# One attention pair ahead: moving the sliding-window attention of a hybrid decoder layer in front of the recurrence it used to run beside

## The chip, the cores and the metric

The kernel runs on one core of a Trainium2 chip. Its time is the device time of one execution in microseconds (us); three runs of the kernel before gave 2196.97, 2198.31 and 2198.78, so a median of 2198.31. The engines are PE (TensorE: matrix multiplications and transposes), DVE (VectorE), ACT (ScalarE), POOL (GpSimd) and SP (SyncE, which here only issues DMAs). Each works through its own queue in order, and semaphores tie them together. A change of 0.2% of the time, 4.4 us, is about what the measurement can tell from none.

## The reference

One layer on 2048 positions of width 1024, in float32. Two groups of heads read the same normed input and are concatenated; a gated MLP with a causal convolution follows.

```python
u = rmsnorm(h, norm_mix_w)
proj = u @ w_in
# 4 recurrent heads (HGRN2) of width 128: q, f, value, output gate
f = lb + (1 - lb) * sigmoid(hf);  k = 1 - f
S_t = diag(f_t) S_{t-1} + k_t v_t^T;  o_t = S_t^T q_t
o_hg = rmsnorm(o, hg_norm_w) * silu(hg)
# 8 attention heads of width 64 (2 key/value heads), window of 128, a sink logit each
o_att = softmax over own and previous 128-key block, plus sink
h = h + concat(o_hg, o_att) @ w_out
v = rmsnorm(h, norm_ffn_w)
gate = causal_depthwise_conv(v @ w_gate)
h = h + (silu(gate) * (v @ w_up)) @ w_down
out = rmsnorm(h, final_norm_w)
```

## The kernel before

The 2048 positions are worked through in two halves of 1024 (`hf`), one after the other. In each half come the mixer (recurrent heads and attention), the output projection (`out_proj`, matrix products into tiles named `pop`), gate and up, and down. Activations lie transposed, channels on the 128 partitions. A float32 product is made of three products of fp32r parts (high by high, high by low, low by high), so each operand is split: ACT casts the high part (`XH`, `whi`), DVE subtracts it for the low part (`XL`, `wlo`). A projection of the input onto 128 channels is one `unit` (line 212): 48 matmuls of 512 columns into two PSUM banks. The products of the recurrence and of the attention proper are float32 or transposes.

The mixer loops over four steps `h`, and each step has a recurrent head (`hgrn`) and a pair of attention heads (`attend`). Both are generators: the loop in the main program calls `next` on the two of them in a written order, and that order is the program's order.

- `attend` first makes its queries (unit `q`, tile `att`); then, for each of two groups of 512 positions, scores (`psc`, line 459) that ACT copies and DVE merges under a mask (`sc`), maximum, exponentials on ACT, division on DVE; then transposes (`ppt`, line 495), masks on DVE (`po`, `pp`, line 498) and the product with the values (`poT`, line 506). It stops (`yield`) after the queries, after both groups' exponentials, and after each group's product.
- `hgrn` makes f and q (units `f`, `hq`), the diagonal of the decay-weighted scores (`pdiag`, line 544), and then seven levels m = 1, 2, 4, ... 64. Each level multiplies on PE (`plev`, lines 569, 602, 607), after which DVE updates Q and K (lines 609, 610) for the next level, copies the level's block into the score matrix ST (lines 585, 625) and halves f (line 616). Then K is transposed (`pkn`, line 640, copied by ACT as `Kn`), the chunk states are made (`pu`, line 647; SS on DVE), the gate unit `g` and the outputs `po` (lines 665, 666), their norm (lines 164 to 176, 674), and transposes `pot` (line 679), after which DVE finishes the head's tile `hg` (line 680).

In steps 0 to 2 a head's `plev` reads K from a copy (`KK`, made by ACT), so that K can be updated while PE works. In the last step (h = 3) it reads K itself, which DVE may then write only once PE has read it.

The last step is special in another way: there is no later head whose units can run beside it. What runs instead is the output projection. `M` holds the eight split tiles that it multiplies (`split`, lines 223 and 224; indices 0 to 3 are the recurrent heads, 4 to 7 the attention pairs), and it takes them in the order 0, 4, 1, 5, 2, 6, 7, 3. Its first output tiles (d = 0, 1, 2) go into PSUM while the last head is still at work. The third may begin only behind `pu` (the table BEHIND):

```python
BEHIND = {1: {0: 1}, 2: {0: "pu", 2: "po", 5: "pot"}}
```

The final order on each engine is set by a scheduler when the program is built. It keeps the program's order as priority and fills an engine's free time with later instructions whose inputs should be there; on the chip each engine then keeps strictly to that list.

Of the kernel before, what the change touches and what calls it, by code (L numbers as in the profile page):

```python
# [8 lines left out]
F32 = mybir.dt.float32  # L9
# [4 lines left out]
ALU = mybir.AluOpType  # L14
# [11 lines left out]
HG = 4  # L26
ATT_J = 4
# [23 lines left out]
def hymba_layer(ctx: ExitStack, tc: tile.TileContext, a: dict, out: bass.AP):  # L51
    nc = tc.nc
# [22 lines left out]
    def halves():  # L75
        return [(b, slice(b * 512, (b + 1) * 512)) for b in range(NB)]
# [138 lines left out]
    def new_x():  # L215
        return (xp.tile([P, HALF], F32R, tag="xh", name="XH", bufs=KT),
                xp.tile([P, HALF], F32R, tag="xl", name="XL", bufs=KT))
# [74 lines left out]
    def slot(name):  # L292
        return hp.tile([P, HALF], F32, tag="m", name=name, bufs=KT)
# [102 lines left out]
    def rows(kv):  # L396
        return slice(kv * HD, (kv + 1) * HD)
# [32 lines left out]
    def attend(hf, j, X, invb, KS, V, mix, p):  # L430

        o = unit(a["w_att"][j], X, "q")
        qT = slot(f"att{j}")
        for b, bs in halves():
            nc.vector.scalar_tensor_tensor(qT[:, bs], o[b], 0.125, invb[:, bs], op0=ALU.mult, op1=ALU.mult)
            nc.scalar.activation(qT[:, bs], qT[:, bs], AF.Identity, bias=C.bq[:, j:j + 1])
        yield
        scs = []
        for g in range(NB):
            sc = p.tile([P, 2, 4, P], F32, tag="sc", name="sc", bufs=2)  # L440
            gs = slice(g * 512, (g + 1) * 512)
            for kv in range(2):
                r, other = rows(kv), rows(1 - kv)

                qh, ql = [p.tile([P, 512], F32R, tag="pp", name=n, bufs=4) for n in ("qh", "ql")]
                nc.scalar.copy(qh[r], qT[r, gs])
                nc.scalar.copy(qh[other], qT[r, gs])
                nc.vector.tensor_tensor(ql[r], qT[r, gs], qh[r].bitcast(F32), op=ALU.subtract)
                nc.scalar.copy(ql[other], ql[r].bitcast(F32))
                for i0 in (0, 2):  # L450
                    pb = ps("at", "psc")
                    first = hf == 0 and g == 0 and i0 == 0
                    for i in range(2):
                        n = g * 4 + i0 + i
                        w0 = 1 if first and i == 0 else 0
                        o = pb[:, i * 256 + w0 * P:(i + 1) * 256]
                        ks = slice((n + w0) * P, (n + 2) * P)
                        for t, qx in enumerate((qh, ql)):
                            nc.tensor.matmul(o, qx[:, (i0 + i) * P:(i0 + i + 1) * P], KS[:, kv, ks],
                                             start=t == 0, stop=t == 1)  # L460
                    pv = pb.rearrange("p (i w k) -> p i w k", i=2, w=2)
                    dst = sc[:, kv, i0:i0 + 2]
                    if first:
                        nc.vector.memset(dst[:, 0], NEG)
                        nc.scalar.copy(dst[:, 1], pv[:, 1, 0])
                    else:
                        nc.scalar.copy(dst, pv[:, :, 0])
                    nc.vector.copy_predicated(
                        dst, C.own.bitcast(U32).unsqueeze(1).to_broadcast([P, 2, P]), pv[:, :, 1])
            m = p.tile([P, 2, 4], F32, tag="mx", name="m", bufs=2)  # L470
            nc.vector.tensor_reduce(m.rearrange("p a b -> p (a b)"),
                                    sc.rearrange("p a b c -> p (a b) c"), axis=AX.X, op=ALU.max)
            sk = C.sinkb[:, j].unsqueeze(2).to_broadcast([P, 2, 4])
            nc.vector.tensor_tensor(m, m, sk, op=ALU.max)
            es = p.tile([P, 2, 4], F32, tag="es", name="es", bufs=2)
            nc.vector.tensor_tensor(es, sk, m, op=ALU.subtract)
            nc.vector.tensor_scalar(m, m, -1.0, None, op0=ALU.mult)
            den = p.tile([P, 2, 4], F32, tag="den", name="den", bufs=2)
            for kv in range(2):
                for i in range(4):  # L480
                    nc.scalar.activation(sc[:, kv, i], sc[:, kv, i], AF.Exp, bias=m[:, kv, i:i + 1],
                                         accum_out=den[:, kv, i:i + 1])
            nc.scalar.activation(es, es, AF.Exp)
            nc.vector.tensor_tensor(den, den, es, op=ALU.add)
            nc.vector.reciprocal(den, den)
            nc.vector.tensor_tensor(sc, sc, den.unsqueeze(3).to_broadcast([P, 2, 4, P]), op=ALU.mult)
            scs.append(sc)
        yield
        for g, sc in enumerate(scs):
            pm = []  # L490
            for kv in range(2):
                pm.append([p.tile([P, 4, P], F32, tag="pp", name=n, bufs=4) for n in ("po", "pp")])
                pt = ps("at", "ppt")
                for i in range(4):
                    nc.tensor.transpose(pt[:, i * P:(i + 1) * P], sc[:, kv, i], ident)
                ptv = pt.rearrange("p (i q) -> p i q", i=4)
                for dst, mk in zip(pm[kv], (C.ownT, C.prevT)):
                    nc.vector.tensor_tensor(dst, ptv, mk.unsqueeze(1).to_broadcast([P, 4, P]), op=ALU.mult)
            oT = ps("at", "poT")
            for i in range(4):  # L500
                n = g * 4 + i
                noprev = hf == 0 and n == 0
                for prev in range(1 if noprev else 2):
                    for kv in range(2):
                        r = rows(kv)
                        nc.tensor.matmul(oT[r, i * P:(i + 1) * P], V[:, n + 1 - prev, r], pm[kv][prev][:, i],
                                         start=prev == 0, stop=noprev or prev == 1)
            gs = slice(g * 512, (g + 1) * 512)
            if j < ATT_J - 1:
                nc.scalar.copy(qT[:, gs], oT)  # L510
                mix[4 + j] = qT
            else:
                if g == 0:
                    mix[4 + j] = new_x()
                h, l = mix[4 + j]
                nc.scalar.copy(h[:, gs], oT)
                nc.vector.tensor_tensor(l[:, gs], oT, h[:, gs].bitcast(F32), op=ALU.subtract)
            yield

    def hgrn(hf, h, X, invb, vs, WG, mix, p, fu=None):  # L520
# [664 lines left out]
    X = []  # L1185
    *nxt, summed = X, *head(X)
    for hf in range(NH):
        X, kv, invb, rs, f0 = nxt
        with ExitStack() as st:
            p = pool(f"mix{hf}", stack=st, reuse_waits="tile")  # L1190
            KS, V = att_keys(hf, kv, invb, p)
            mix = [None] * KT
            vs = []
            M, WG = {}, {}
            for h in range(HG):
                hg = hgrn(hf, h, X, invb, vs, WG, mix, p, f0 if h == 0 else None)
                at = attend(hf, h, X, invb, KS, V, mix, p)
                with tc.issue_after(summed.ins) if hf + h == 0 else ExitStack():
                    next(hg)
                if h == HG - 1:  # L1200
                    next(at)
                    next(hg)
                    for kt in (0, 4, 1, 5, 2, 6):
                        M[kt] = split(mix[kt])
                    next(hg)
                elif h % 2 == 0:
                    next(at)
                    wv = [prep(a["w_v"][h // 2, s]) for s in range(2)]
                    next(hg)
                    vs += project_v(hf, wv, X, rs, p)  # L1210
                else:
                    next(hg)
                    next(at)
                if h < HG - 1:
                    WG[h] = prep(a["w_g"][h])
                next(at)
                next(hg)
                if h < HG - 1:
                    next(hg)
                next(at)  # L1220
                if h < HG - 1:
                    next(at)
                    next(hg)
                else:
                    next(hg)
                    next(at)
            M[7], M[3] = mix[7], mix[3]
        with ExitStack() as st:
            p = pool(f"ffn{hf}", stack=st, reuse_waits="tile")
            kept, ops, hs, first, last = out_proj(hf, M, p)  # L1230
            acts = gate_up(hf, ops, hs, first, last, p)
            nxt = down(hf, kept, acts, p)
# [61 lines left out]
```

## Time and profile before

| what | value |
|---|---|
| median of three runs | 2198.31 us (2196.97 to 2198.78) |
| profiled execution, first to last instruction | 2198.0 us |
| mean granted TensorE clock | 0.997 |
| PE busy | 2180.4 us (99%), 11424 matmuls |
| DVE busy | 1639.5 us (75%) |
| ACT busy | 1049.9 us (48%) |
| mixer with the overlapped start of the output projection, first half | about 47 to 402 us |
| the same, second half | about 1136 to 1492 us |

A row of the time line gives the start, the time from the first start to the last end, the engine, line, operation and tiles, and how many instructions were merged; a bracket names an idle time before it and what ended it. Matmuls overlap in the array, so the mean duration of one (389 ns at 512 columns) is longer than the distance between two starts (0.23 us), and the distance is what counts in a sum. For the same reason "PE busy" holds short waits. A float32 matmul stands as two records, so eight `plev` instructions are x16. In the table of windows the columns are the stretch, its length and the busy time of PE, weight loads, DVE, ACT and POOL with their instructions; then the granted clock, the DMA share and GB/s.

### The profile page before, as it was taken

The page shows a single profiled execution, that of the slowest core. Times are in us where ns is not written, and L with a number is a line of the kernel's source. Part 1 is how long each engine was busy: PE and PEld are TensorE (multiplying, and loading weights), DVE is VectorE, ACT ScalarE, POOL GpSimd, SP SyncE. Part 2 cuts the span into 40 slices and gives each one's busy share as a digit, 9 for nine tenths or more (in the row PEclk, how much of TensorE's full clock was granted, in tenths as well). Part 3 has the DMA queues.
Part 4 walks back from the last instruction along what each step waited for, and adds up shares of the span by engine and source line. Part 5 has one row for each costly group of instructions (what it writes and reads, how often), then busy time and mean ns, then how long its engine had stood idle before and what let it go on. Part 6 is the DMA issues. An engine that isn't in the chain of part 4 may idle for free.

```text
span 2198.0 us, 29524 instructions
## 1 busy us (share of the span) xinstructions
PE 2180.4 (99%) x11424; PEld 1834.0 (83%) x11424; DVE 1639.5 (75%) x2451; ACT 1049.9 (48%) x1848; POOL 6.3 (0%) x28
## 2 busy tenths in 40 slices
PE   9999999999999999999999999999999999999998
PEld 7988988888888888888889889888888888888888
DVE  6567568688887888885855666677888878887766
ACT  6445544454444445335735455544644444443353
POOL 1000000000000000000000000000000000000000
PEclk9999999999999999999999999999999999999999
DMA  4101112323333234964631111114132323259643
GB/s 155 51 32 48 39 41 68 119 74 102 104 109 108 89 127 143 372 241 156 209 125 41 44 36 51 58 39 134 58 125 92 125 91 109 98 183 393 233 144 130
DMA packets 94358, 257.91 MB, mean 117 GB/s; under 512 B 11594, under 2 KB 17546, under 8 KB 94218
## 3 DMA queue, kind: packets, MB, share of 16 engines
q1 hardware_dynamic: 88992, 251.30, 33.9%
q10 hardware_dynamic: 5226, 4.73, 0.7%
q8 instruction: 89, 1.46, 0.3%
q14 instruction: 51, 0.42, 0.1%
HBM read 195.10 MB, written 57.15 MB: 115 GB/s over the span
## 4 chain that ended last, share of the span: by engine, by line
PE 95%; DVE 3%; ACT 1%; DMA 1%; issue 0%; SPq 0%; DVEq 0%; ACTq 0%
PE X L877 7%; PE X L878 7%; PE X L879 7%; PE pop L212 7%; PE hq L212 4%; PE q L212 4%; PE f L212 4%; PE g L212 4%; PE Y L879 4%; PE Y L878 4%; PE Y L877 4%; PE pdx L1088 3%; PE pdx L1089 3%; PE pdx L1090 3%; PE pdy L1089 3%; PE pdy L1088 3%
## 5 line engine op out<-in xcount | busy, mean ns | idle before, releaser
L706 ACT CAST whi<-raw 128x1024 fp32r<-128x1024 f32 x88 | 92.6, 1053 | 109.2 <-PE X L878 68.2
L877 PE MATMUL X<-T,whi 128*128 128x512 f32 x352 | 136.9, 389 | 0.0
L878 PE MATMUL X<-T,whi 128*128 128x512 f32 x352 | 136.9, 389 | 0.0
L879 PE MATMUL X<-T,wlo 128*128 128x512 f32 x352 | 136.9, 389 | 0.0
L972 DVE SCALAR_TENSOR_TENSOR y<-ga,cw,y 128x1024 f32<-128x1024 f32 x88 | 112.5, 1281 | 26.0 <-ACT y L970 26.0
L884 ACT COPY u<-X 128x512 f32<-128x512 f32 x88 | 51.4, 585 | 133.3 <-PE X L879 133.1
L707 DVE TENSOR_TENSOR wlo<-raw,whi 128x1024 fp32r<-128x1024 f32 x88 | 107.3, 1220 | 0.0
L190 ACT CAST whi<-raw 128x1024 fp32r<-128x1024 f32 x57 | 59.5, 1048 | 93.1 <-PE q L212 31.9
L707 DVE TENSOR_TENSOR xld<-raw,xhd 128x1024 fp32r<-128x1024 f32 x72 | 80.8, 1133 | 19.1 <-ACT xhd L706 18.9
L706 ACT CAST xhd<-raw 128x1024 fp32r<-128x1024 f32 x72 | 69.7, 978 | 43.6 <-DMA raw<-act0T 14.8
L212 PE MATMUL pop<-XL,whi 128*128 128x512 f32 x256 | 86.1, 396 | 2.1 <-DVE XL L224 2.1
L212 PE MATMUL pop<-XH,wlo 128*128 128x512 f32 x256 | 85.2, 393 | 0.8 <-DVE wlo L191 0.8
L212 PE MATMUL pop<-XH,whi 128*128 128x512 f32 x256 | 84.5, 397 | 0.2
L878 PEld LDWEIGHTS X<-T,whi 128*128 128x128 f32 x352 | 66.1, 188 | 13.7
L877 PEld LDWEIGHTS X<-T,whi 128*128 128x128 f32 x352 | 66.1, 188 | 13.7
L879 PEld LDWEIGHTS X<-T,wlo 128*128 128x128 f32 x352 | 66.1, 188 | 13.7
L1088 PE MATMUL pdx<-xhd,hid 128*128 128x512 f32 x192 | 74.4, 391 | 1.0 <-ACT hid L706 1.0
L1089 PE MATMUL pdx<-xld,hid 128*128 128x512 f32 x192 | 74.7, 389 | 0.0
L1090 PE MATMUL pdx<-xhd,lod 128*128 128x512 f32 x192 | 73.7, 389 | 0.0
L698 PE MATMUL pvv<-whi,XH 128*128 128x256 f32 x256 | 73.5, 288 | 0.0
L191 DVE TENSOR_TENSOR wlo<-raw,whi 128x1024 fp32r<-128x1024 f32 x57 | 69.5, 1222 | 4.2 <-ACT whi L190 4.1
L699 PE MATMUL pvv<-whi,XL 128*128 128x256 f32 x256 | 72.6, 284 | 0.0
(379 smaller groups left out, 6563.3 us busy)
## 6 DMA issues: line engine op xcount, KB each, us to landing
wr<-in_w_down SPq DMA_DIRECT2D x90, 512.0 KB, 4.8
raw<-in_w_gate SPq DMA_DIRECT2D x44, 512.0 KB, 3.6
raw<-in_w_up SPq DMA_DIRECT2D x44, 512.0 KB, 3.6
raw<-act0T SPq DMA_DIRECT2D x20, 512.0 KB, 6.1
raw<-act1T SPq DMA_DIRECT2D x20, 512.0 KB, 10.1
act0B<-y SPq DMA_DIRECT2D x33, 256.0 KB, 2.6
act1B<-y SPq DMA_DIRECT2D x33, 256.0 KB, 2.4
raw<-in_w_out SPq DMA_DIRECT2D x16, 512.0 KB, 4.7
```

The costliest lines, as they stand in the source:

```text
L212: marks["unit"] = nc.tensor.matmul(o[b], w, x[:, bs], start=f, stop=l)
L698: nc.tensor.matmul(o[:, 0:256], xh[:, t], hi[:, c], start=kt == 0, stop=False)
L699: nc.tensor.matmul(o[:, 0:256], xl[:, t], hi[:, c], start=False, stop=False)
L706: return (nc.scalar.copy(h, src), (eng or nc.vector).tensor_tensor(l, src, h.bitcast(F32), op=ALU.subtract))
L707: (eng or nc.vector).tensor_tensor(l, src, h.bitcast(F32), op=ALU.subtract))
L877: nc.tensor.matmul(o, wh[:, ws], xh, start=i == 0 and not more, stop=False, skip_group_check=more)
L878: nc.tensor.matmul(o, wh[:, ws], xl, start=False, stop=False, skip_group_check=more)
L879: r = nc.tensor.matmul(o, wl[:, ws], xh, start=False, stop=i == 3, skip_group_check=more)
L972: nc.vector.scalar_tensor_tensor(y, g[:, w:w + HALF], C.cw[:, ft, w:w + 1], y, op0=ALU.mult, op1=ALU.add)
L1088: nc.tensor.matmul(o, wh[:, i, c], ah[:, i, cols], start=f, stop=False, skip_group_check=more)
L1089: nc.tensor.matmul(o, wh[:, i, c], al[:, i, cols], start=False, stop=False, skip_group_check=more)
L1090: nc.tensor.matmul(o, wl[:, i, c], ah[:, i, cols], start=False, stop=l, skip_group_check=more)
```

## The change

The four attention generators are made at the start of a half and run one step ahead. Step 0 takes pair 0 and all of pair 1, interleaved; steps 1 and 2 take pairs 2 and 3; step 3 takes none. The output of pair 3 is written to its tile `att` like the others (line 509 in the program after) and split with the rest (index 7 in the list of the last step), where before it was split straight from PSUM in two halves (lines 516 and 517).

```diff
@@ attend
-            if j < ATT_J - 1:
-                nc.scalar.copy(qT[:, gs], oT)
-                mix[4 + j] = qT
-            else:
-                if g == 0:
-                    mix[4 + j] = new_x()
-                h, l = mix[4 + j]
-                nc.scalar.copy(h[:, gs], oT)
-                nc.vector.tensor_tensor(l[:, gs], oT, h[:, gs].bitcast(F32), op=ALU.subtract)
+            nc.scalar.copy(qT[:, gs], oT)
+            mix[4 + j] = qT
             yield
@@ main program
+            at = [attend(hf, j, X, invb, KS, V, mix, p) for j in range(ATT_J)]
             for h in range(HG):
                 hg = hgrn(hf, h, X, invb, vs, WG, mix, p, f0 if h == 0 else None)
-                at = attend(hf, h, X, invb, KS, V, mix, p)
                 with tc.issue_after(summed.ins) if hf + h == 0 else ExitStack():
                     next(hg)
                 if h == HG - 1:
-                    next(at)
                     next(hg)
-                    for kt in (0, 4, 1, 5, 2, 6):
+                    for kt in (0, 4, 1, 5, 2, 6, 7):
                         M[kt] = split(mix[kt])
-                    next(hg)
-                elif h % 2 == 0:
-                    next(at)
+                    for _ in range(3):
+                        next(hg)
+                    break
+                own = at[h + 1] if h else at[0]
+                if h != 1:
+                    next(own)
+                if h % 2 == 0:
                     wv = [prep(a["w_v"][h // 2, s]) for s in range(2)]
-                    next(hg)
+                next(hg)
+                if h == 1:
+                    next(own)
+                if h % 2 == 0:
                     vs += project_v(hf, wv, X, rs, p)
-                else:
-                    next(hg)
-                    next(at)
-                if h < HG - 1:
-                    WG[h] = prep(a["w_g"][h])
-                next(at)
+                WG[h] = prep(a["w_g"][h])
+                next(own)
+                if h == 0:
+                    next(at[1])
                 next(hg)
-                if h < HG - 1:
-                    next(hg)
-                next(at)
-                if h < HG - 1:
-                    next(at)
-                    next(hg)
-                else:
-                    next(hg)
-                    next(at)
-            M[7], M[3] = mix[7], mix[3]
+                next(hg)
+                next(own)
+                next(own)
+                if h == 0:
+                    next(at[1])
+                next(hg)
+                if h == 0:
+                    next(at[1])
+                    next(at[1])
+            M[3] = mix[3]
```

No matmul is added or removed (10446 in both programs). What the change does to the built lists is seen best in the last step. This is PE's list of the first half before, around the levels m = 16 and 32 of head 3 (`ppt` and `poT` are pair 3's attention, `pop` the output projection):

```order
L495 MATMUL ppt<-ident,sc 128x128 x4
L602 MATMUL plev<-Q,K 128x64 x8
L212 MATMUL pop_3557<-XH,whi 128x512
L212 MATMUL pop_3626<-XH,whi 128x512
L495 MATMUL ppt<-ident,sc 128x128 x4
L506 MATMUL poT<-po,V 64x128
L212 MATMUL pop_3557<-XL,whi 128x512
L212 MATMUL pop_3557<-XH,wlo 128x512
L212 MATMUL pop_3626<-XL,whi 128x512
L212 MATMUL pop_3626<-XH,wlo 128x512
L607 MATMUL plev<-Q,K 32x32 x16
```

Between every two levels stood attention or output projection. This is PE's list now at the same place, from level m = 4 on (lines 595, 600, 633 and 640 are 602, 607, 640 and 647 of before; `pop_3697` is the third output tile):

```order
L212 MATMUL pop_3627<-XL,whi 128x512
L212 MATMUL pop_3627<-XH,wlo 128x512
L595 MATMUL plev<-Q,K 128x64 x24
L600 MATMUL plev<-Q,K 32x32 x16
L600 MATMUL plev<-Q,K 64x64 x8
L633 MATMUL pkn<-ident,K 128x128 x8
L640 MATMUL pu<-v,Kn 128x128 x8
L212 MATMUL pop_3697<-XH,whi 128x512
L212 MATMUL pop_3698<-XH,whi 128x512
```

Levels 4, 8 and 16 (x24), 32, 64, the transposes and `pu` now follow each other with nothing between. The second half has the same rows. On DVE the same place read before, from level m = 8 on:

```order
L625 COPY_PREDICATED ST<-lmask_324,plev 128x64x8
L609 TENSOR_TENSOR Q<-Q,f 128x64x8
L610 TENSOR_TENSOR K<-K,f 128x64x8
L616 TENSOR_TENSOR f<-f 128x64
L498 TENSOR_TENSOR po<-ppt,ownT 128x512
L498 TENSOR_TENSOR pp<-ppt,prevT 128x512
L517 TENSOR_TENSOR XL<-poT,XH 128x512
L609 TENSOR_TENSOR Q<-Q,f 128x32x16
L610 TENSOR_TENSOR K<-K,f 128x32x16
L625 COPY_PREDICATED ST<-lmask_328,plev 128x32x16
L616 TENSOR_TENSOR f<-f 128x32
```

and reads now:

```order
L602 TENSOR_TENSOR Q<-Q,f 128x64x8
L603 TENSOR_TENSOR K<-K,f 128x64x8
L618 COPY_PREDICATED ST<-lmask_324,plev 128x64x8
L609 TENSOR_TENSOR f<-f 128x64
L602 TENSOR_TENSOR Q<-Q,f 128x32x16
L603 TENSOR_TENSOR K<-K,f 128x32x16
L618 COPY_PREDICATED ST<-lmask_328,plev 128x32x16
L609 TENSOR_TENSOR f<-f 128x32
L602 TENSOR_TENSOR Q<-Q,f 128x16x32
L603 TENSOR_TENSOR K<-K,f 128x16x32
L609 TENSOR_TENSOR f<-f 128x16
```

The attention's masks and its split have left the levels, and only the recurrence's own four operations for each level remain. The attention rows stand in steps 0 to 2 instead, among the units of those steps. On SP's queue the fetches of query weights of pairs 1 to 3 stand one step earlier among the other weights in each half (three such fetches in a half stand in other places, and none comes between the last step's weights). On ACT the program has 23 table loads where it had 27.

## Prediction

> **What bounds the kernel now.** I read the page's busy table first, then the table of 10 us windows over the mixer, then PE's rows one by one where its share dips.
>
> ```profile
> PE 2180.4 (99%) x11424; PEld 1834.0 (83%) x11424; DVE 1639.5 (75%) x2451; ACT 1049.9 (48%) x1848; POOL 6.3 (0%) x28
> 110.00:120.00 10.00, 10.00 (x58) 8.70 (x57) 7.59 (x17) 9.62 (x27) 0.00 (x0) 1.00 0.00 0
> 340.00:350.00 10.00, 9.65 (x71) 8.64 (x69) 8.60 (x14) 6.16 (x12) 0.00 (x0) 1.00 0.22 66
> 350.00:360.00 10.00, 9.30 (x51) 8.00 (x51) 9.47 (x20) 5.96 (x25) 0.00 (x0) 1.00 0.32 100
> 360.00:370.00 10.00, 9.32 (x71) 8.07 (x71) 9.84 (x18) 2.49 (x14) 0.00 (x0) 0.91 0.00 0
> 370.00:380.00 10.00, 10.00 (x124) 8.36 (x120) 7.75 (x17) 2.18 (x5) 0.00 (x0) 0.92 0.01 2
> ```
>
> PE is the bound: 99% of the span. In steps 0 to 2 (110 to 120 us stands for them) it is full, and DVE has room there. In the last step of the first half, 340 to 380 us, PE has small holes, DVE is nearly full, and the granted clock, 1.00 elsewhere, falls to 0.91 and 0.92. So the kernel is a list of PE work plus a few us of PE waiting in two last steps, and a change that keeps every matmul can act only on that waiting and on the clock. I take as the unit of account the stretch from head 2's `pot` to head 3's `pkn`, once in each half:
>
> ```profile
> 341.37 1.04 PE L679 MATMUL pot<-ident,on 128*128 128x128 f32 x8
> 381.65 1.07 PE L640 MATMUL pkn<-ident,K 128*128 128x128 f32 x8
> 1431.28 1.03 PE L679 MATMUL pot<-ident,on 128*128 128x128 f32 x8
> 1471.72 1.06 PE L640 MATMUL pkn<-ident,K 128*128 128x128 f32 x8
> ```
>
> It lasts 40.28 us in the first half and 40.44 us in the second.
>
> **What leaves the stretch.** Pair 3's products stand in it, by PE's groups in this window and, for the pace, four other rows:
>
> ```profile
> L506 PE MATMUL poT<-po,V 128*64 128x128 f32 x32 | 5.6, 336 | 0.0
> L506 PE MATMUL poT<-pp,V 128*64 128x128 f32 x28 | 5.1, 341 | 0.0
> L459 PE MATMUL psc<-KS,qh 128*128 128x256 f32 x9 | 2.5, 299 | 0.0
> L459 PE MATMUL psc<-KS,ql 128*128 128x256 f32 x9 | 2.3, 280 | 0.0
> L495 PE MATMUL ppt<-ident,sc 128*128 128x128 f32 x16 | 2.5, 290 | 0.0
> L544 PE MATMUL pdiag<-hg,K 128*128 128x128 f32 x16 | 2.3, 288 | 0.3 <-DVE hg L680 0.3
> 1432.39 0.28 PE L459 MATMUL psc<-KS,qh 128*128 128x256 f32 x1
> 1432.51 0.28 PE L459 MATMUL psc<-KS,ql 128*128 128x256 f32 x1
> 374.36 0.44 PE ppt L495 x4
> 376.92 1.89 PE poT L506 x29
> ```
>
> The chain's rows end where the next begins, so they give the pace: 0.11 us for a `ppt`, 0.065 for a record of `poT`; starts of `psc` lie 0.12 apart. 18 x 0.12 + 16 x 0.11 + 60 x 0.065 = 7.8 us. This work isn't saved. It moves to steps 0 to 2, where PE has no free tenth, and there it costs its full 7.8 us in each half.
>
> **What the stretch costs without it.** By PE's new list it holds `pot`, `pdiag`, seven levels and 60 `pop` (2 + 37 + 21), with 16 more between head 2's last `po` and its `pot`. The paces:
>
> ```profile
> 334.71 0.62 PE L212 MATMUL pop<-XL,whi 128*128 128x512 f32 x2
> 335.17 0.62 PE L212 MATMUL pop<-XH,wlo 128*128 128x512 f32 x2
> 391.84 0.39 PE L666 MATMUL po<-SS,Q 128*128 128x128 f32 x2
> 396.18 1.03 PE L679 MATMUL pot<-ident,on 128*128 128x128 f32 x8
> 1433.10 1.97 PE L544 MATMUL pdiag<-hg,K 128*128 128x128 f32 x16
> 346.72 1.90 PE L602 MATMUL plev<-Q,K 128*128 128x64 f32 x16
> 348.43 0.73 PE L212 MATMUL pop<-XL,whi 128*128 128x512 f32 x2
> 376.22 0.70 PE L607 MATMUL plev<-Q,K 128*32 128x32 f32 x32
> 287.01 1.15 PE L607 MATMUL plev<-Q,K 128*64 128x64 f32 x16
> ```
>
> Two `pop` start 0.46 us after the two before, 0.227 each in longer runs. Head 3's outputs take 4.34 us from the last `po` to `pot` (391.84 to 396.18), through the norm. If head 2's take the same, 16 `pop` fill 3.63 and the `po` itself 0.22, which leaves a wait of 0.5 ahead of `pot`. Then come `pot` with the 0.3 us wait for `hg` (1.3), `pdiag` (1.97 less the 0.18 by which its last one overlaps the next start: 1.79), 60 x 0.227 = 13.6, and levels 1 and 2 at 1.71 each (346.72 to 348.43): 20.1 us.
>
> From level 4 on nothing stands between the levels. A level reads Q and K; when PE has read them DVE writes Q, then K, and only then may PE begin the next. What a level costs behind PE, by the chain and one row of DVE:
>
> ```profile
> 364.40 0.60 DVE Q L609
> 365.00 0.61 DVE K L610
> 365.62 0.14 issue
> 380.82 0.69 DVE L610 TENSOR_TENSOR K<-K,f 128x512 f32<-128x512 f32 x1
> ```
>
> Levels 4, 8 and 16: 1.90 on PE, 0.02 to DVE's start, 0.60 for Q, 0.69 for K to its end, 0.14 back: 3.35 each, 10.05 in all. From level 32 to 64: 0.70 + 1.45 = 2.15. From 64 to `pkn`: 1.15 + 1.45 = 2.60. Together 14.8 us, of which PE waits about 7.8.
>
> So the stretch takes 0.5 + 20.1 + 14.8 = 35.4 us, 8.6 of it waits. With the 7.8 us moved, the half gains 35.4 + 7.8 - 40.28 = +2.9 us, in the second half +2.8. Said otherwise: without attention the work is 26.8 us, so before some 5.7 us of the stretch were lost, and now 8.6 will be. Sum at full clock: +5.7 us.
>
> **The clock.** The trace has two short drops, each just behind a window with holes:
>
> ```profile
> 364.85:368.26 3.41, 2.73 (x25) 2.26 (x24) 3.41 (x8) 0.00 (x0) 0.00 (x0) 1.00 0.00 0
> 368.26:371.67 3.41, 3.41 (x28) 2.75 (x25) 2.62 (x6) 0.28 (x1) 0.00 (x0) 0.50 0.00 0
> 1436.62:1440.04 3.42, 2.03 (x15) 1.73 (x15) 3.42 (x5) 2.29 (x5) 0.00 (x0) 1.00 0.16 65
> 1440.04:1443.45 3.41, 3.41 (x9) 2.63 (x9) 3.41 (x7) 0.00 (x0) 0.00 (x0) 0.50 0.69 166
> 347.78:351.19 3.41, 2.71 (x16) 2.08 (x16) 3.41 (x6) 0.60 (x1) 0.00 (x0) 1.00 0.44 125
> 1440.70 1.05 PE L212 MATMUL pop<-XH,wlo 128*128 128x512 f32 x2
> ```
>
> A window with PE busy 2.03 of 3.42 (0.59) was followed by half clock, so was one at 0.80, another at 0.79 was not. At half clock a pair of `pop` shows 1.05 instead of 0.62. The new levels make 1.90 busy in 3.35 us, a share of 0.57 for three levels on end, below the lower of the two. Each level is a window long, so I expect the clock to fall after about one (level 4) and stay down until a window is full, which comes in `pu`. At half clock PE's part doubles and DVE's doesn't: level 16 +1.7, level 32 +0.6, level 64 +1.1, `pkn` +0.8, `pu` 0 to +1.8: 4.2 to 6.0. I take 5.0 a half, near the middle. The ends are 0 (no drop) and 10.4 (from level 8 through `pu` and the first twelve `pop`: 1.7 and 2.7 more on top of 6.0). Two halves: +10.
>
> The Trainium skill, "TensorE: Matmul & The Clock Gate", section "HAM oscillation — how this bites in real kernels", asks only that PE should have no idle gap of about a whole window, 3.4 us. By that rule alone gaps of 1.45 us would leave the clock up, and the time would be the 2204.0 of the first rival below; the two drops shown, behind windows in which PE worked 59% and 80%, speak against it. Its section "A second HAM failure mode: psum-queue depth-cycling" names frequent short idle times as enough, and the trace agrees.
>
> **Costed at nothing.** Pair 3's output is now split like the others: one subtract of 1024 columns in place of two of 512 from PSUM (0.69 each), done by DVE under the 60 `pop`; were that cover gone, it would be some 1.3 us ahead of index 7's products. DVE's moved masks and merges lie where its window reads 7.59 of 10 or less; without that room the rival on steps 0 to 2 holds. Four table loads less on ACT and the two projection casts less: ACT ends no wait there. The weight fetches that move up on SP find a DMA share of 0.00 in the mixer's window and come earlier, never later, than needed. POOL has no part in it.
>
> **Sum.** 2198.0 (profiled span) + 5.7 + 10 = 2213.7. The median stands 0.3 above the profiled execution: 2214.0.
>
> **Rivals.**
> 1. *The clock stays up.* For it: the window at 0.79 without a drop. Against: two drops at higher or like shares than 0.57. Then only the waits count: 2198.3 + 5.7 = 2204.0.
> 2. *The clock stays down through the whole end of the step.* If it falls after the first holes and recovers only behind the twelve `pop`, 10.4 a half: 2198.3 + 5.7 + 20.8 = 2224.8.
> 3. *Steps 0 to 2 begin to wait.* DVE and ACT get a pair more in step 0, where the window has ACT at 9.62. A level's update that comes late behind attention's merges would cost 1.2 us (one `sc`-sized operation) at a time; I allow 4 us in all: 2218.
> 4. *Faster: the scheduled list keeps PE full.* If the waits of a half's stretch fell below 5.7 us instead of 8.6, the change would gain; the mechanism would be that DVE, relieved of attention, answers each level sooner than its 1.45 us and PE, 1.9 us behind with `pop`, reaches level 4 only when later ones are ready. With none of them left it is -5.7 - 5.8: 2198.3 - 11.5 = 2186.8. Against: from level 4 on PE's list has no `pop` to wait behind, and Q and K take their 0.60 on an idle DVE too.
> 5. *No net change.* Busy PE rows hide short waits. If the 7.8 us that moves filled such waits for 2.8 us a half, and the clock stayed up, 2204.0 - 5.6 = 2198.4.
>
> **How the numbers follow.** Forecast 0.50, with a range of its own of 2209 to 2219 (clock 2.5 to 7.5 a half); rival 1 0.15; rival 2 0.15; rival 3 0.05; rival 4 0.07; rival 5 0.08. The range 2203 to 2226 takes in the forecast and rivals 1 to 3, 0.85, and leaves out 4 and 5. Slower by over 0.2% (4.4 us, about what a measurement here can tell from no change): 0.85; within 0.2%: 0.08; faster: 0.07.
>
> **What would show it.** Right: the stretch at about 35 us plus what the clock adds, so the first half's `pkn` near 389.6 if the clock falls first at level 16 or behind (381.65 + 2.9, and 1.7 to 5 more); idle times ahead of levels 8 to 64 and `pkn` that name DVE's K; the granted clock at 0.50 in one or two windows of 3.4 us there; windows in steps 0 to 2 still at 10.00 for PE. Wrong: levels closer than 3.3 us on end, `pop` rows between them, a clock of 1.00 throughout, or new PE waits in steps 0 to 2.

## The result and the profile after

The changed kernel takes 2220.21 us (median of four runs, 2218.76 to 2221.72) where the kernel before takes 2198.55. The quotient of these two medians is 1.0099; the ratio estimated from the runs is 1.0102, with a 95% interval of 1.0087 to 1.0116. It is slower, inside the range of 2203 to 2226 and 6.2 us above the forecast of 2214.0. The profiled execution has a span of 2217.0 us, 19.0 more than before.

The page's busy line and the two 10 us windows of the first half's last step that changed most, after (columns as above):

```profile
PE 2186.2 (99%) x11424; PEld 1841.1 (83%) x11424; DVE 1641.0 (74%) x2449; ACT 1048.1 (47%) x1846; POOL 6.0 (0%) x28
370.00:380.00 10.00, 7.04 (x49) 6.67 (x47) 4.26 (x8) 0.00 (x0) 0.00 (x0) 0.81 0.00 0
380.00:390.00 10.00, 5.57 (x60) 5.14 (x61) 4.88 (x10) 1.42 (x4) 0.00 (x0) 0.50 0.00 0
```

The share of PE over the whole span still reads 99%. The loss shows in these two windows of ten microseconds, where PE works 70% and 56% of the time, DVE is no longer full either (4.26 and 4.88 of 10), and the clock is at 0.81 and 0.50: neither engine is full, they wait for each other. PE's rows there, from the time line (the bracket is the idle time before the row and what ended it), and the second half's `pkn`:

```profile
349.44 1.31 PE L672 MATMUL pot<-ident,on 128*128 128x128 f32 x8 [0.50 <-DVE on L667]
364.20 1.89 PE L595 MATMUL plev<-Q,K 128*128 128x64 f32 x16
370.80 1.89 PE L595 MATMUL plev<-Q,K 128*128 128x64 f32 x16
374.17 1.97 PE L595 MATMUL plev<-Q,K 128*128 128x64 f32 x16 [1.48 <-DVE K L603]
377.61 3.64 PE L595 MATMUL plev<-Q,K 128*128 128x64 f32 x16 [1.48 <-DVE K L603]
382.74 1.07 PE L600 MATMUL plev<-Q,K 128*32 128x32 f32 x32 [1.48 <-DVE K L603]
385.28 1.94 PE L600 MATMUL plev<-Q,K 128*64 128x64 f32 x16 [1.48 <-DVE f L609]
388.70 1.94 PE L633 MATMUL pkn<-ident,K 128*128 128x128 f32 x8 [1.48 <-DVE K L603]
...
1489.27 1.94 PE L633 MATMUL pkn<-ident,K 128*128 128x128 f32 x8 [1.48 <-DVE K L603]
```

Levels 4, 8 and 16 start at 370.80, 374.17 and 377.61, 3.4 us apart, with 1.48 us of waiting before each of the last two. From level 16 on PE's rows are longer than at full clock (3.64 us for 1.97 at level 16, 1.07 for 0.70 at level 32, 1.94 for 1.06 at `pkn`), while the waits stay at 1.48: that is the clock. The chain shows what the 1.48 us consist of:

```profile
370.96 1.75 PE plev L595 x16
372.70 0.02 issue
372.73 0.69 DVE Q L602
373.42 0.61 DVE K L603
374.03 0.14 issue
```

And the clock's own windows, ahead of the drop, the drop and its last window, then the same of the second half without the last:

```profile
372.77:376.18 3.41, 1.97 (x16) 1.86 (x16) 2.16 (x5) 0.00 (x0) 0.00 (x0) 1.00 0.00 0
376.18:393.25 17.07, 11.20 (x85) 10.54 (x86) 7.52 (x16) 2.48 (x5) 0.00 (x0) 0.50 0.00 0
389.83:393.25 3.42, 3.42 (x17) 3.14 (x16) 0.58 (x2) 1.17 (x2) 0.00 (x0) 0.50 0.00 0
1471.86:1475.27 3.41, 1.93 (x18) 1.82 (x17) 2.19 (x4) 0.00 (x0) 0.00 (x0) 1.00 0.00 0
1475.27:1492.34 17.07, 11.16 (x86) 10.30 (x86) 6.95 (x14) 2.48 (x5) 0.00 (x0) 0.50 0.00 1
```

One window with PE busy 1.97 of 3.41 us (0.58), and the clock halves for 17.07 us, five windows, in both halves alike. In the first half it comes back behind a window that is full (3.42 of 3.42), in the second behind one with PE busy 3.06 of 3.41.

Where the 19.0 us of the two profiles came from, stretch by stretch (from the rows' starts; loss is a stretch less its matmuls at the paces of the prediction):

| stretch | before, us | after, us | loss before | loss after |
|---|---|---|---|---|
| 1st half: first matmul to head 2's `pot` | 340.3 | 348.3 | 13.1 | 13.8 |
| its `pot` to head 3's `pkn` | 40.28 | 39.26 | 6.4 | 12.8 |
| `pkn` to head 3's `pot` | 14.53 | 16.35 | 1.5 | 3.3 |
| from there to head 2's `pot` of the 2nd half | 1035.1 | 1044.4 | 14.5 | 15.6 |
| its `pot` to `pkn` | 40.44 | 39.81 | 5.7 | 13.1 |
| `pkn` to `pot` | 14.53 | 15.62 | 1.5 | 2.6 |
| the rest | 705.3 | 705.6 | 5.5 | 6.0 |

The two last steps, up to head 3's `pot`, lose 16.7 us more than before; everything else together 2.3 more.

### The profile page after: what moved, and what is told of

Its sections match the earlier page's. It is cut to its first block, busy times and chain, and to the rows that moved or that the text cites. A ratio compares the mean times of both kernels' runs of the same rounds, so it can differ in the third digit from the quotient of the medians.

```text
span 2217.0 us, 29542 instructions
## 1 busy us (share of the span) xinstructions
PE 2186.2 (99%) x11424; PEld 1841.1 (83%) x11424; DVE 1641.0 (74%) x2449; ACT 1048.1 (47%) x1846; POOL 6.0 (0%) x28
## 4 chain that ended last, share of the span: by engine, by line
PE 96%; DVE 2%; issue 1%; DMA 1%; ACT 0%; SPq 0%; DVEq 0%; ACTq 0%
PE pop L212 7%; PE X L870 7%; PE X L871 7%; PE X L872 7%; PE f L212 4%; PE hq L212 4%; PE g L212 4%; PE q L212 4%; PE pdx L1081 4%; PE pdx L1083 4%; PE Y L872 4%; PE Y L871 4%; PE Y L870 4%; PE pdx L1082 4%; PE pdy L1081 3%; PE pdy L1083 3%
## 5 line engine op out<-in xcount | busy, mean ns | idle before, releaser
L602 DVE TENSOR_TENSOR Q<-Q,f 128x512 f32<-128x512 f32 x56 | 38.8, 692 | 59.6 <-PE plev L595 24.4
```

## The experiments

My theory: PE's list leaves the last head's levels bare, so PE waits 1.48 us for DVE at each of them, and these waits pull the clock down. The main rival: the attention that moved into steps 0 to 2 makes those steps wait, and the bare levels are harmless. A second question is how the loss divides between the waits and the clock.

**Filling the levels with real work.** The changed kernel, with the second output tile's products held back behind the levels (`marks` for levels 32 and 64 are set too):

```diff
-BEHIND = {1: {0: 1}, 2: {0: "pu", 2: "po", 5: "pot"}}
+BEHIND = {1: {0: 1, 2: 4, 3: 8, 4: 16, 5: 32, 6: 64}, 2: {0: "pu", 2: "po", 5: "pot"}}
```

> The second output tile's products are held back so that six pop stand behind each of the levels 2 to 64 of the last head, where they stood ahead of level 4; attention stays one step ahead. Theory (the loss is made by the empty gaps of the last head): the stretch from head 2's pot to head 3's pkn falls from 39.3 and 39.8 us to about 29, the clock stays at 1.00, time 2194 to 2199. Rival (the attention that moved into steps 0 to 2 costs the time): 2212 or more, whatever stands in the gaps.

Measured: 2196.26 us, 0.9989 of the kernel before (0.9980 to 0.9998). The first half's `pot`, PE's rows between levels 8 and 16 (cut at the dots), and `pkn`:

```profile
349.57 1.31 PE L672 MATMUL pot<-ident,on 128*128 128x128 f32 x8 [0.50 <-DVE on L667]
367.72 1.97 PE L595 MATMUL plev<-Q,K 128*128 128x64 f32 x16
369.50 0.71 PE L212 MATMUL pop<-XH,whi 128*128 128x512 f32 x2
...
371.17 1.97 PE L595 MATMUL plev<-Q,K 128*128 128x64 f32 x16
379.45 1.06 PE L633 MATMUL pkn<-ident,K 128*128 128x128 f32 x8
```

A level still takes 3.45 us (367.72 to 371.17), but six `pop`, 1.4 us, now stand in it. Nothing about attention differs from the changed kernel, and 24 us are gone: the stretch went from 39.26 to 29.88 us and from 39.81 to 29.82, with no drop of the clock in either. The rival falls.

**Holding the clock without shortening the waits.** Matmuls without use (128 columns, on an idle PSUM bank) behind each of levels 4 to 64 of the last head, first twelve, then six, two and four:

```diff
+            if h == HG - 1 and m >= 4:
+                without_use(ps("at", "fill"), FILLERS, marks[m])
```

> Twelve matmuls without use stand behind each of levels 4 to 64 of the last head, 1.3 us in a gap of 1.45 us; nothing else changes. Theory (level waits and a falling clock share the loss, about 10 us of it the clock in the two halves): the clock stays at 1.00, levels come every 3.4 us, the pkn of the first half some 3 us earlier, time 2208 to 2212. Rival (the clock costs nothing that the waits don't, or the loss lies in steps 0 to 2): 2218 to 2222.

Measured: 2220.32 us (1.0099, 1.0084 to 1.0114), what the rival expected, but not for its reason:

```profile
372.32 2.90 PE L95 MATMUL fill<-ones 128*128 128x128 f32 x24
375.06 1.90 PE L596 MATMUL plev<-Q,K 128*128 128x64 f32 x16
```

Each float32 matmul stands as two records, and the twelve take 2.74 us from start to the next level, not 1.3. They hold PE for 1.1 us beyond each gap (a level takes 4.46 us instead of 3.4). The clock did stay at 1.00, and the 10 us it gave were spent on the filling: 5 gaps x 1.1 x 2 = 11. The run was mis-sized and is repeated with six.

> As the run with twelve matmuls without use behind each level, with six: twelve took 2.57 us, six take 1.29 us and fit the gap of 1.48 us. Theory (a falling clock is some 5 us of each half's loss): granted clock 1.00 in both last steps, stretches of 35 to 36 us instead of 39.3 and 39.8, time 2208 to 2212. Rival (the waits are all, the clock's fall costs nothing beside them): 2218 to 2222.

Measured: 2209.99 us (1.0053, 1.0038 to 1.0069). The first half's `pot`, a level's filling and the next level, `pkn`, and the time in which the changed kernel had its drop:

```profile
351.11 1.10 PE L675 MATMUL pot<-ident,on 128*128 128x128 f32 x6 [0.50 <-DVE on L670]
374.15 1.56 PE L95 MATMUL fill<-ones 128*128 128x128 f32 x12
375.79 1.97 PE L596 MATMUL plev<-Q,K 128*128 128x64 f32 x16
387.47 1.06 PE L636 MATMUL pkn<-ident,K 128*128 128x128 f32 x8
375.00:392.00 17.00, 16.46 (x165) 15.19 (x164) 10.25 (x23) 2.38 (x5) 0.00 (x0) 1.00 0.00 1
```

The levels come as late as before, and PE does nothing more for the result; only the clock stays up. So of the 21.7 us, 10.2 are the clock and 11.5 are not.

> Two matmuls without use behind each of levels 4 to 64 instead of six: 0.43 us of the 1.48 us gap, so PE shows about 2.33 busy in a level of 3.38 us (0.69). Theory (the clock falls behind windows in which PE's share is low, and the shares seen before a drop were 0.59 and 0.80): it still falls in both halves, 2214 to 2221. Rival (only the length of a single gap counts, and 1.05 us is short enough): 2208 to 2212.

> Four of them: 0.86 us of the gap, PE 2.76 busy in 3.38 us (0.82). Theory: above the shares seen before a drop, so the clock stays at 1.00 or falls for a single window, 2208 to 2213. Rival (the gaps must be filled whole): the drop stays, 2214 to 2221.

Measured: with two, 2218.14 us (1.0085, 1.0068 to 1.0101); with four, 2209.47 us (1.0049, 1.0035 to 1.0063). The window ahead of the drop and the drop with two, then the same place with four:

```profile
372.59:376.01 3.42, 2.44 (x23) 2.28 (x21) 1.60 (x3) 0.00 (x0) 0.00 (x0) 1.00 0.00 0
376.01:389.66 13.65, 12.29 (x87) 11.43 (x87) 6.26 (x14) 0.72 (x2) 0.00 (x0) 0.50 0.00 0
```

```profile
372.50:375.90 3.40, 2.87 (x26) 2.71 (x25) 2.20 (x4) 0.00 (x0) 0.00 (x0) 1.00 0.00 0
375.00:392.00 17.00, 14.87 (x145) 13.40 (x145) 9.79 (x23) 2.38 (x5) 0.00 (x0) 1.00 0.00 1
```

With PE busy 0.71 of the window the clock fell in both halves, though no gap was longer than 0.98 us, so the rival falls; with 0.84 it didn't fall. The four executions with two lie 8 us apart, at a mean granted clock of 0.991 to 0.996, so the drop isn't equally long in each; the profiled one took 2220.04 us. Fewer matmuls lower the share and lengthen the gaps together, so these two runs don't tell which of them the clock follows, and the last section shows that neither alone sorts the windows.

**One half alone.** Attention ahead in the first half (`if hf == AHEAD`, with AHEAD = 0), the second as in the kernel before:

> Attention one step ahead in the first half of the positions alone; the second half as in the kernel before. Theory (each half's last step makes its own loss): half of the 21.7 us, 2208 to 2211, the second half's stretch at 40.4 us with no long clock drop. Rival (the loss comes from carrying on, a clock or a queue that the first half leaves behind): outside 2205 to 2214.

Measured: 2209.97 us (1.0053, 1.0039 to 1.0067). The second half's stretch is 40.0 us, as before:

```profile
1441.39 1.03 PE L680 MATMUL pot<-ident,on 128*128 128x128 f32 x8
1481.41 1.07 PE L641 MATMUL pkn<-ident,K 128*128 128x128 f32 x8
```

Half of the change makes half of the loss, 11.6 us in the median for one half and 21.7 for two, and the second half carries nothing on from the first.

**The price of the moved work.** In `attend`, pair 3 ends behind its exponentials (`mix[7]` is then its queries):

```diff
+        if j == ATT_J - 1:
+            mix[4 + j] = qT
+            yield
+            yield
+            return
```

> Left out: pair 3's transposes, masks and products with the values (the output projection then reads its queries). In the changed kernel these stand in step 2. Theory (PE is full there, so moved work costs its full duration): 16 x 0.11 + 60 x 0.065 = 5.7 us a half less, 2207 to 2211, with the last step and its clock as before. Rival (steps 0 to 2 had room, the loss is all in the last step): 2218 to 2221. Rival (steps 0 to 2 wait on DVE or ACT for attention): under 2205.

Measured: 2212.43 us (1.0064, 1.0047 to 1.0081), 7.8 us under the changed kernel and 1.4 above the range expected. In the second half the moved work costs its full price and more: head 1's `pot` to head 2's takes 83.72 us instead of 91.45, 7.7 less for 5.9 us of matmuls at the prediction's paces (16 `ppt` and, in this half, 64 records of `poT`). In the first half the same distance is only 2.0 shorter, because without pair 3's products the list set 16 `pop` ahead of head 2's last `po` instead of behind them:

```profile
347.50 1.97 PE L677 MATMUL pot<-ident,on 128*128 128x128 f32 x8 [4.13 <-DVE on L672]
342.91:346.32 3.41, 0.46 (x4) 0.26 (x3) 2.64 (x10) 0.37 (x2) 0.00 (x0) 1.00 0.00 0
346.32:353.15 6.83, 5.66 (x25) 5.26 (x26) 4.71 (x9) 2.87 (x4) 0.00 (x0) 0.50 0.00 0
```

The head's norm, 4.1 us that `pop` covers elsewhere, stood bare, and the clock fell there as well. So the work isn't free where it stands now. In the second half it costs 1.8 us beyond its matmuls, and no idle row of PE names DVE or ACT for that; its exact price in the first half stays open.

**Giving the levels back their attention.** Pair 3's two products in step 3 again, behind levels 4 and 16:

```diff
+                    with tc.issue_after(marks[4].ins):
+                        next(at[3])
+                    with tc.issue_after(marks[16].ins):
+                        next(at[3])
```

> Only pair 3's transposes, masks and products come back into the last head's levels (behind levels 4 to 32); queries, scores and exponentials stay one step ahead. Theory: the 5.7 us of work a half leave steps 0 to 2 and fall into gaps that PE spends waiting; with nothing left ahead of pkn and masks between DVE's level updates some waits stay: 2199 to 2209, clock drops shorter or none. Rival (the moved work costs nothing where it stands now): 2218 or more.

Measured: 2214.13 us (1.0071, 1.0056 to 1.0086), better than the changed kernel by 6 us, but 5 us above the range expected. Two reasons stand in the rows:

```profile
347.74 1.95 PE L672 MATMUL pot<-ident,on 128*128 128x128 f32 x8 [4.13 <-DVE on L667]
381.07 0.40 PE L506 MATMUL poT<-po,V 128*64 128x128 f32 x2 [1.20 <-DVE f L609]
```

The bare norm of head 2 is here too, in the first half, and attention is a poor filler: its products wait for masks that DVE, in order, writes behind the level's updates (1.20 us ahead of `poT`), so they fill a gap and open another.

**The same aid on the kernel before.** The spread table with attention where it was:

> The kernel before, with attention where it was, and the second output tile's products held back so that six pop stand behind levels 2 to 16 and a few behind 32 and 64, beside pair 3's products. Theory (in the kernel before the levels wait for a DVE that is full with attention's merges, masks and splits, so more pop between them mend little): 2194 to 2200, the stretch 38 to 41 us. Rival (any even spread of pop is the gain, attention's place doesn't matter): 2188 or less.

Measured: 2198.18 us, 0.9998 (0.9989 to 1.0007). The stretch is 38.15 and 37.80 us. DVE is full there, and a level waits 1.26 us:

```profile
350.00:360.00 10.00, 9.02 (x57) 7.82 (x58) 10.00 (x20) 5.06 (x20) 0.00 (x0) 1.00 0.29 96
361.88 1.97 PE L602 MATMUL plev<-Q,K 128*128 128x64 f32 x16 [1.26 <-DVE es L476]
358.05 1.20 DVE L471 TENSOR_REDUCE m<-sc 128x8 f32<-128x1024 f32 x1
361.03 0.70 DVE L610 TENSOR_TENSOR K<-K,f 128x512 f32<-128x512 f32 x1
```

The bracket names `es`, a small attention operation that ended last, but `plev` reads Q and K: K's update ends at 361.73, late because attention's maximum (`m`, 1.20 us) stood ahead of it on DVE. So moving attention out of the last step does remove a limit, DVE's; the change lost because it removed the fillers of PE with it. With the spread table alone the gain from attention's place is 1.9 us in the medians and the intervals overlap; the last experiment parts them.

**Answering a level in two parts.** The kernel with spread `pop`, and in the last head DVE updates Q and K of half the positions, then of the other half:

```diff
+            for b in ([slice(0, nb // 2), slice(nb // 2, nb)] if h == HG - 1 else [slice(0, nb)]):
+                fs = [b.stop - b.start, m]
...
```

> The kernel with spread pop and attention ahead, in which DVE updates Q and K of the last head in two parts of half the positions each, so that PE may start a level on the first part. Theory (what is left of the loss, 3.3 us a half, is mostly the rest of the level's answer that six pop don't cover, some 0.2 us at six places, and 0.7 at pot and pdiag): 1 to 1.5 us less a half, 2193 to 2196. Rival (more, smaller operations on DVE make it late in the first levels): 2196 to 2200.

> The kernel before, attention where it was, with both aids of the best kernel so far: pop spread over the levels and Q and K updated in two parts. Theory (there DVE is full in the last step, and more operations on it don't help): 2195 to 2200, no faster than 2195, so that attention one step ahead is what makes room for the gain. Rival (attention's place is neutral, the two aids are all): 2191 to 2194.5, at or under the kernel with attention ahead and the same aids.

Measured: with attention ahead 2194.25 us, 0.9984 of the kernel before (0.9975 to 0.9992); with attention where it was 2199.06 us, 1.0002 (0.9994 to 1.0011). With attention ahead the stretch is 28.89 and 28.83 us:

```profile
349.52 1.32 PE L674 MATMUL pot<-ident,on 128*128 128x128 f32 x8 [0.50 <-DVE on L669]
378.41 0.82 PE L635 MATMUL pkn<-ident,K 128*128 128x128 f32 x6
```

That is 1.0 us a half less than with whole updates. The interval overlaps that of the spread kernel, but not that of the same aids with attention where it was, which is 4.8 us slower. Both versions with attention ahead lie under the kernel before, with intervals below 1, though by less than the 4.4 us named at the start; this is the fastest version found.

## Why the prediction was right

*The bound and the place.* Right. The loss is in the two last steps, 16.7 of 19.0 us, and steps 0 to 2 took the moved work at its price: head 2's `pot` comes 8.1 us later in the first half, for a forecast of 7.8. The run with spread `pop` shows that the place decides.

*The stretch at full clock.* The mechanism was right, the size too small. The 35.4 us hold a wait of 0.5 ahead of `pot`, which lies in front of the stretch as it was defined and came in the first half alone; without it the forecast is 34.9, and the run with six fillers has 36.36 and 36.31. The five waits behind levels are 1.48 us each (1.45 forecast), 7.4 in all; the prediction's "about 7.8" is not the sum of its own five, 7.25, but only the remark on what was lost before and rival 4 use it. What was missed lies mostly at the front. The distance from level 1 to level 2 is 10.91 us (353.29 to 364.20) where 37 `pop` and a level make 10.1: PE waits for a split on DVE.

```profile
353.29 1.89 PE L595 MATMUL plev<-Q,K 128*128 128x64 f32 x16
356.94 0.73 PE L212 MATMUL pop<-XL,whi 128*128 128x512 f32 x2 [0.32 <-DVE XL L224]
355.67 2.35 DVE L224 TENSOR_TENSOR XL<-att,XH 128x1024 fp32r<-128x1024 f32 x2
```

The two splits on DVE are those of indices 6 and 7, in that order, and PE goes on when the first of them ends. So the late one is index 6, which the kernel before waited for as well (0.70 and 1.39 us there); the prediction priced the 60 `pop` at their pace and left this wait out. The moved split, index 7, stands behind it, and PE shows no wait for it: that it costs nothing was right.

*The clock.* The step that carried most of the forecast, and it came out: forecast 10 us in two halves, 10.2 by the runs (2220.21 to 2209.99), 9.3 by the profiles. The drop began at level 16 and ended in `pu`, as worked out. The first half's `pkn` stands at 388.70, for 389.6, which is partly luck: 389.6 counts all 5.0 us of the clock ahead of `pkn`, where by the prediction's own rows only 3.4 lie there (388.0), and the front of the stretch took longer than forecast. The drop lasted five windows of 3.41 us and not one or two, as the prediction's last part had it. The cost was summed over the rows that the drop covers, not over windows, and so didn't suffer. That a share of 0.57 must bring the clock down was argued from fewer windows than the trace has: the kernel before has a third drop, at 1108.95 us, behind a window that PE's rows fill, and other runs have single windows at 0.47 to 0.63 without one (last section). What the runs bear out is that several bare levels on end bring it down.

*The rule that spoke against it.* The Trainium skill, "TensorE: Matmul & The Clock Gate", section "HAM oscillation — how this bites in real kernels", would have the clock stay up, since the longest gap was 1.48 us. The trace contradicts it: the drops stand behind windows that PE filled to 0.58 and 0.71. Its section "A second HAM failure mode: psum-queue depth-cycling" names frequent short idle times as enough, there from cycling PSUM banks; the trace agrees that they are enough behind the bare levels, where they are waits for DVE.

*What was left out.* The forecast is 6.2 us low. The stretches with the wait ahead of `pot` account for 2.4 (1.5 in the first half, 0.9 in the second). Small losses elsewhere, 1.8 us beside that wait, were given to rival 3 and not to the sum; no idle row of PE names their cause, and they stay open. Against these, the clock in the profile cost 0.7 less than taken. The moved products were miscounted by little: two of the 18 `psc` start ahead of the first half's stretch, and the second half has 64 records of `poT`, not 60, which makes 7.6 and 7.8 us instead of 7.8 twice, 0.2 less. The rest is in the last term: the prediction set the median 0.3 us above the profiled span, from one pair of numbers, but in the runs since a profiled execution lasts 1.7 us longer than its span (2218.76 and 2217.0 for the changed kernel), and this one was the shortest of its four, 1.45 under the median. Together 3.2 instead of 0.3. The terms make 2.4 + 1.8 - 0.7 - 0.2 + 2.9 = 6.2.

*The rivals.* Rival 1 (the clock stays up) gave 2204.0; the run that makes it so measured 2209.99, so its sum was low by the same omissions. Rival 2 (the clock stays down up to the twelve `pop`) fell: it came back in `pu`. Of rival 3 (steps 0 to 2 begin to wait) at most the 1.8 us of small losses are left. Rival 4 (PE never waits, 2186.8) needed `pop` behind the levels; the runs that put them there measured 2196.26 and 2194.25, faster than before but not by 11 us, since some 2.4 to 3.3 us a stretch and 1.5 behind it stay lost. Rival 5 fell: PE's full windows in steps 0 to 2 held no room for the moved work.

## What to carry to other kernels

Work on a second engine that looks like a burden on the last step may be what PE lives on there: before moving it away, see what PE's list has left between two dependent levels, and hold back independent work for each of them. A PE that works in short bursts can pay twice, once for the waits and once for the clock, and here the second bill was almost as large as the first (10.2 of 21.7 us). Read the share in windows of a few microseconds: over the whole span it stood at 99% before and after.

## What the runs showed of the hardware

In every profile that leaves the levels bare, or with two matmuls of no use each, one after another, the clock fell behind the first such window of 3.4 us: in both halves of the changed kernel, in the changed half of the run with one half alone, in both halves without pair 3's products, and in both with two such matmuls a level. PE showed 0.57 to 0.71 busy in these windows, with no single gap above 1.48 us, and the clock stayed at 0.50 for four to six windows. With four, six or twelve matmuls a level (0.84 busy with four) it fell in none. Four leave 0.53 of the 1.48 us idle and are cheaper than the drop by 10 us; more than the gap holds costs all that it gains.

The busy share of one window doesn't decide it by itself. The rows are, in order: the run with one half alone, in its unchanged second half; the kernel before with both aids; and two of the kernel before.

```profile
1447.40:1450.82 3.42, 2.03 (x12) 1.60 (x12) 3.42 (x5) 1.61 (x4) 0.00 (x0) 1.00 0.02 7
355.25:358.66 3.41, 1.61 (x8) 1.00 (x7) 3.41 (x7) 2.61 (x14) 0.00 (x0) 1.00 0.00 0
1105.53:1108.95 3.42, 3.42 (x26) 3.18 (x26) 2.83 (x15) 0.00 (x0) 0.00 (x0) 1.00 1.01 377
1108.95:1112.36 3.41, 3.41 (x10) 2.63 (x9) 3.31 (x15) 1.04 (x1) 0.00 (x0) 0.50 0.12 44
```

The first two, at 0.59 and 0.47, were followed by full clock; the first stands at the place where the kernel before, at the same 0.59, lost it. The last two show the clock halved behind a window that PE's rows fill, half of it with products of a single column (`pst`, 1106.37 to 1108.07 us); nine of the thirteen profiles have such a drop near there. So the profile's busy share isn't quite what the clock follows, and what it is stays open, as does the way back: at half clock a full window didn't bring it back with two matmuls a level (376.01 to 379.42 us), and one at 0.91 did.
